# Small transfers of two mixers moved from a shared pair of DMA queues to GpSimd's alone, with their consumers one step later

## The chip, the cores and the metric

The kernel runs on one core of a Trainium2 chip. The metric is the time of one execution on the device in microseconds, the median of several runs. A profile of one execution goes with it: the instructions of every engine with their times, the DMA transfers, and what each engine waited for.

## The reference

The program computes two layers of a decoder trunk for one sequence of 256 tokens of width 2048, in float32. Cut to what matters here:

```python
def reference(x, ...):
    for l in range(DEPTH):                       # DEPTH = 2
        h = rms_norm(x, mix_norm[l])
        h = mixer_ab(h, ...) if l % 2 == 0 else mixer_c(h, ...)
        x = x + h
        h = rms_norm(x, ffn_norm[l])
        x = x + conv_ffn(h, ffn_w_up[l], ffn_conv_w[l], ffn_conv_b[l], ffn_w_down[l])
    return x

def mixer_ab(h, w_in, ...):                      # gMLP heads and HGRN2 heads side by side
    u, v, q, f, i, g = jnp.split(h @ w_in, cuts, axis=-1)
    ...
    return jnp.concatenate([y_a, y_b], axis=-1) @ w_out

def mixer_c(h, w_in, ...):                       # attention with forgetting, 16 heads
    q, k, v, g, f = jnp.split(h @ w_in, ..., axis=-1)
    ...
    return o @ w_out

def conv_ffn(h, w_up, conv_w, conv_b, w_down):
    z = h @ w_up
    z = sum(conv_w[j] * zp[:, j:j + seq] for j in range(CONV_WIDTH)) + conv_b
    a, b = jnp.split(z, 2, axis=-1)
    return (jax.nn.silu(a) * b) @ w_down
```

Nearly all the arithmetic is in the projections `h @ w`. The weights, over 400 MB, are read once.

## The kernel before, in words

**Weights.** Every projection streams its weights in blocks of 512 KB. `weights` (calls `three`, a DMA on SP's queue at L181, and `halves`) brings a block into `w`. ScalarE then writes its rounded half `wh` (L175), VectorE the rest `wl` (L176). The matmuls use both halves of weights and of activations, three products in place of one, which keeps float32's accuracy. Four buffers of `w` and three each of `wh` and `wl` turn over (two more of each in the feed-forward parts), so SP's queue and the two engines work a few blocks ahead of TensorE.

**Steps.** `project_four` (L311 to L313) and `project_tok` (L292 to L294) take two of 16 slices of the model's width for each weight block: 12 matmuls, one *step*. At each step they call `tick`, which moves every running generator one `yield` on. All other work is written as generators: they wait a number of steps with bare `yield`s and then record their instructions. `LAG = 6` is the usual number of steps between a block's transfers and its first reader. `depth` limits how many generators run at once; the others wait in `queue`. The recorded program goes through a scheduler, which sets each engine's order within the dependencies and the extra ones that `held` and `tied` add ("not before this weight split", "not before this matmul").

**Turned blocks.** `project_four` gives tokens on the partitions and features along the row; what follows needs the reverse. `blocks` (L324) transposes 32 x 32 squares with two instructions of VectorE into `tmp`, and `moves` (L331) puts the squares into their places with 16 DMAs of 32 KB within SBUF, from `tmp` to the block's destination. `transposed` does both. The 16 DMAs alternate between SP's queue, where the weights also are, and GpSimd's. A queue issues in order, so a transfer that waits for `tmp` holds up what stands behind it.

**Who uses them.** In `mixer_ab`: `gates` (two blocks `turn`, from the projection f, for the hgrn heads), `gated` (two blocks written into `o`), `spatial` (two blocks `turn`, from the projection u), and `add_four` (four blocks `dst`, the rows of the output projection, added to `xT`). In `mixer_c`: queries and keys of four groups (eight blocks `turn`, read by `attend` at L949), `gate` (four), and `add_four` again (four). In `ffn` every block `zt` goes the same way. Between gates and output, `hgrn` (one generator for each of eight heads) keeps ScalarE and VectorE busy with short instructions while TensorE streams the projections q and i.

**Also on GpSimd's queue**: the copies `ar` (L283, reversed activations for the projection i), and in `mixer_c` the store `cd` (L928) and four loads `cb` (L934), which spread the sums of the forget gates over the partitions; `attend` reads `cb` at L958 and L960.

**Feeding the next part.** `add_four`'s generator adds the turned row to `xT` and calls `nxt.feed`, which makes the activations of the next norm. The last row (`q == 3`) waits two steps less than the others, as the feed-forward part needs it soon. In the rows 1 and 2 of `mixer_ab` (`halves == 2`) the second half of the 16 transfers is issued one step after the first.

Of the kernel before, what the change touches and what calls it, by code (L numbers as in the profile page):

```python
# [25 lines left out]
LAG = 6  # L26
# [27 lines left out]
def tile_trunk(ctx: ExitStack, tc: tile.TileContext, x, pp_d, cst_d, mlev_d, msk_d,  # L54
               w_v, w_f, w_g, w_i, w_q, w_u, w_abo, w_cf, w_cqkv, w_cg, w_co, w_up, w_dn, spw_d, spb_d, out):
    nc = tc.nc
# [259 lines left out]

    def transposed(src, tmp, dst, queues=(nc.sync, nc.gpsimd)):

        blocks(src, tmp)
        moves(tmp, dst, queues)  # L320
# [5 lines left out]

    def moves(tmp, dst, queues=(nc.sync, nc.gpsimd), rows=range(4)):
        n = 2 * BLK
        for a in rows:
            for b in range(4):  # L330
                queues[(a + b) % len(queues)].dma_start(dst[BLK * b:BLK * (b + 1), :, a * n:(a + 1) * n],  # L331
                                  tmp[BLK * a:BLK * (a + 1), b * 4 * n:(b + 1) * 4 * n]
                                  .rearrange("p (m r) -> p m r", m=4))
# [125 lines left out]

    def add_four(q, ps, z, tmp, dst, nxt, halves=1):  # L460
        for T in range(2):
            SC.activation(z[:, T], ps[T], AF.Copy)
        blocks(lambda T: z[:, T], tmp)
        moves(tmp, dst, rows=range(4 // halves))

        def rest():
            if halves == 2:
                yield
                moves(tmp, dst, rows=range(2, 4))
            for _ in range(LAG - 2 * (q == 3)):  # L470
                yield
            for i in range(4):
                m = 4 * q + i
                held(V.tensor_tensor(xT[m], xT[m], dst[:, i], ALU.add), "wl")
                nxt.feed(m)
                if q < 3 or i % 2:
                    yield
            if q == 3:
                for _ in range(WAIT):
                    yield  # L480
                yield from nxt.finish_tok()

        queue.append(rest())


    def mixer_ab(norm):
# [106 lines left out]
        ps = bank()  # L593
# [29 lines left out]
        def gates(j, z):  # L623

            for _ in range(LAG):
                yield
# [15 lines left out]
        for j in range(2):  # L642
# [4 lines left out]
            t = hp.tile([P, 1024], F32, tag="o", name=nm("turn"), bufs=2)  # L647
            transposed(lambda T: z[:, T * 512:(T + 1) * 512], tmp, t.rearrange("p (m t) -> p m t", m=4))
            queue.append(gates(j, t))
# [118 lines left out]
        def gated(j):  # L768
# [15 lines left out]
            for _ in range(2 * (j == 0)):  # L784
                yield
            moves(tmp, t.rearrange("p (m t) -> p m t", m=4))
            for _ in range(LAG - 1):
                yield
# [22 lines left out]
        def spatial(j, z):  # L811
            for _ in range(LAG):
                yield
# [9 lines left out]
        for j in range(2):  # L823
# [4 lines left out]
            t = hp.tile([P, 1024], F32, tag="tok", name=nm("turn"), bufs=2)  # L828
            transposed(lambda T: z[:, T * 512:(T + 1) * 512], tmp, t.rearrange("p (m t) -> p m t", m=4))
            depth[0] = 4  # L830
# [14 lines left out]
        for q in range(4):  # L845
# [12 lines left out]
            if q == 0:  # L858
                depth[0] = 2
            add_four(q, ps, z, tmp, dst, nxt, 2 if q in (1, 2) else 1)  # L860
        es.close()
# [4 lines left out]
    def mixer_c(norm):  # L866
# [127 lines left out]
        def flat(t):  # L994
            return t.rearrange("p t c -> p (t c)")

        def heads(t):
            return flat(t).rearrange("p (m t) -> p m t", m=4)

        for g in range(CH // 4):  # L1000
            qkv = []
            ss = hp.tile([P, 2, 2, LANE // 4], F32, tag="ss", name=nm("ss"), bufs=2)[..., 0:4]
            for j in range(3):
# [12 lines left out]
                if j < 2:  # L1016
# [5 lines left out]
                    t = piece("turn", 4)  # L1022
                    transposed(lambda T: z[:, T], flat(piece("tmp", 2)), heads(t))
                    z = heads(t)
# [8 lines left out]
        def gate(q, z):  # L1033
# [7 lines left out]
            for _ in range(2 * (q < 2)):  # L1041
                yield
            moves(tmp, heads(t))
            for _ in range(LAG - 2 * (q == 3)):
                yield
# [24 lines left out]
    def ffn(l, norm, last):  # L1070
# [69 lines left out]
        def add_y(q, finish):  # L1140
            tmp, zt = room()
            near = last and q == 2
            transposed(lambda T: y[:, T, q * 512:(q + 1) * 512], tmp, zt,
                       (nc.sync, nc.gpsimd, SC) if near else (nc.sync, nc.gpsimd))

# [155 lines left out]
```

## Time and profile before

| | us |
|---|---|
| median of 3 runs | 2288.69 |
| lowest and highest | 2287.63, 2288.85 |
| span of the profiled execution, first to last instruction | 2287.3 |
| TensorE (PE) busy | 2280.8 |
| weight loads into TensorE (PEld) | 1893.5 |
| VectorE (DVE) busy | 1559.8 |
| ScalarE (ACT) busy | 1309.6 |
| GpSimd (POOL) busy | 361.2 |

The profile gives a span but no time of its own for the whole execution; the difference between the median and the span is 1.4 us. "PE pm L311" is a matmul of TensorE at line 311 that writes the tile `pm`. SP is the engine whose queue issues most of the DMAs; "SPq" and "POOLq" are the sequencers of SP and GpSimd. In the timeline each row has the start in us from the span's start, the duration, and in brackets the idle time of the engine before it with what ended it. In the view of waits the numbers are the total, the count and the longest.

### The profile page before, as it was taken

The page shows a single profiled execution, that of the slowest core. Times are in us where ns is not written, and L with a number is a line of the kernel's source. Part 1 is how long each engine was busy: PE and PEld are TensorE (multiplying, and loading weights), DVE is VectorE, ACT ScalarE, POOL GpSimd, SP SyncE. Part 2 cuts the span into 40 slices and gives each one's busy share as a digit, 9 for nine tenths or more (in the row PEclk, how much of TensorE's full clock was granted, in tenths as well). Part 3 has the DMA queues.
Part 4 walks back from the last instruction along what each step waited for, and adds up shares of the span by engine and source line. Part 5 has one row for each costly group of instructions (what it writes and reads, how often), then busy time and mean ns, then how long its engine had stood idle before and what let it go on. Part 6 is the DMA issues. An engine that isn't in the chain of part 4 may idle for free.

```text
span 2287.3 us, 32261 instructions
## 1 busy us (share of the span) xinstructions
PE 2280.8 (100%) x10832; PEld 1893.5 (83%) x10832; DVE 1559.8 (68%) x2309; ACT 1309.6 (57%) x1980; POOL 361.2 (16%) x662
## 2 busy tenths in 40 slices
PE   9999999999999999999999999999999999999999
PEld 8888888888888888888888888888888888888887
DVE  7788767777467656766875675767776476657766
ACT  7677756666456445654565555655665465456642
POOL 0121221212012002111111111211211012012102
PEclk9999999999999999999999999999999999999999
DMA  8655767778667667776666655777777677667765
GB/s 288 195 169 160 215 199 235 238 216 234 193 208 221 206 201 213 220 213 186 213 227 203 194 177 181 220 224 242 225 217 218 195 216 210 209 205 216 223 204 174
DMA packets 489415, 480.45 MB, mean 210 GB/s; under 512 B 114112, under 2 KB 457168, under 8 KB 489120
## 3 DMA queue, kind: packets, MB, share of 16 engines
q1 hardware_dynamic: 467040, 453.54, 64.2%
q0 software_dynamic: 20480, 22.50, 4.3%
q10 hardware_dynamic: 1728, 2.35, 0.3%
q8 instruction: 85, 1.39, 0.3%
q14 instruction: 82, 0.67, 0.1%
HBM read 435.24 MB, written 2.11 MB: 191 GB/s over the span
## 4 chain that ended last, share of the span: by engine, by line
PE 97%; DVE 2%; ACT 1%; issue 0%; SPq 0%; DMA 0%; DVEq 0%; ACTq 0%
PE pm L311 26%; PE pm L312 26%; PE pm L313 26%; PE pm L292 4%; PE pm L294 4%; PE pm L293 4%; PE pm L193 1%; PE pm L266 1%; PE pm L217 1%; DVE wl L176 0%; PE pm L269 0%; ACT wh L175 0%; DVE kq L701 0%; PE px L955 0%; SPq L331 0%
## 5 line engine op out<-in xcount | busy, mean ns | idle before, releaser
L176 DVE TENSOR_TENSOR wl<-w,wh 128x1024 fp32r<-128x1024 f32 (+1 forms) x820 | 996.9, 1219 | 637.0 <-ACT wh L175 629.3
L175 ACT ACTIVATE wh<-w 128x1024 fp32r<-128x1024 f32 (+1 forms) x820 | 862.5, 1054 | 786.0 <-PE pm L313 552.3
L311 PE MATMUL pm<-wh,a 128*128 128x512 f32 x1728 | 674.4, 390 | 0.0
L312 PE MATMUL pm<-wl,a 128*128 128x512 f32 x1728 | 672.5, 389 | 0.0
L313 PE MATMUL pm<-wh,a 128*128 128x512 f32 x1728 | 672.5, 389 | 0.0
L331 POOL DMA_DIRECT2D zt<-tmp x413 | 223.5, 549 | 1201.6 <-DVE tmp L324 1089.8
L313 PEld LDWEIGHTS pm<-wh,a 128*128 128x128 f32 x1728 | 324.4, 188 | 67.4
L312 PEld LDWEIGHTS pm<-wl,a 128*128 128x128 f32 x1728 | 324.4, 188 | 67.3 <-DVE wl L176 0.5
L311 PEld LDWEIGHTS pm<-wh,a 128*128 128x128 f32 x1728 | 324.4, 188 | 67.1
L311 PE MATMUL pm<-wh,hid 128*128 128x512 f32 x688 | 267.6, 389 | 0.0
L312 PE MATMUL pm<-wl,hid 128*128 128x512 f32 x688 | 267.6, 389 | 0.0
L313 PE MATMUL pm<-wh,hid 128*128 128x512 f32 x688 | 267.6, 389 | 0.0
L331 POOL DMA_DIRECT2D turn<-tmp x160 | 86.7, 550 | 504.5 <-DVE tmp L324 256.7
L292 PE MATMUL pm<-wh,a 128*128 128x512 f32 x416 | 165.2, 397 | 0.0
L294 PE MATMUL pm<-wh,a 128*128 128x512 f32 x416 | 162.1, 390 | 0.0
L293 PE MATMUL pm<-wl,a 128*128 128x512 f32 x416 | 162.0, 389 | 0.0
L311 PEld LDWEIGHTS pm<-wh,hid 128*128 128x128 f32 x688 | 129.2, 188 | 26.9
L313 PEld LDWEIGHTS pm<-wh,hid 128*128 128x128 f32 x688 | 129.2, 188 | 26.8
L312 PEld LDWEIGHTS pm<-wl,hid 128*128 128x128 f32 x688 | 129.2, 188 | 26.7
L1105 ACT ACTIVATE conv<-zt,pp 128x256 f32<-128x256 f32 x176 | 95.9, 589 | 26.1 <-DMA zt<-tmp 22.2
L324 DVE STREAM_TRANSPOSE tmp<-z 128x512 f32<-128x512 f32 x120 | 83.4, 704 | 18.9 <-ACT z L1091 18.4
L294 PEld LDWEIGHTS pm<-wh,a 128*128 128x128 f32 x416 | 78.1, 188 | 16.6
(244 smaller groups left out, 2075.6 us busy)
## 6 DMA issues: line engine op xcount, KB each, us to landing
w<-in_w_up SPq DMA_DIRECT2D x352, 512.0 KB, 4.4
w<-in_w_dn SPq DMA_DIRECT2D x176, 512.0 KB, 4.5
w<-in_w_cqkv SPq DMA_DIRECT2D x96, 512.0 KB, 4.3
w<-in_w_abo SPq DMA_DIRECT2D x32, 512.0 KB, 4.6
w<-in_w_cg SPq DMA_DIRECT2D x32, 512.0 KB, 4.3
w<-in_w_co SPq DMA_DIRECT2D x32, 512.0 KB, 4.3
zt<-tmp SPq DMA_DIRECT2D x414, 32.0 KB, 2.7
zt<-tmp POOLq DMA_DIRECT2D x413, 32.0 KB, 2.5
```

What stands on the lines that cost most here:

```text
L175: r = deep["wh"] = SC.activation(wh, w, AF.Copy)
L176: deep["wl"] = V.tensor_tensor(wl, w, wh.bitcast(F32), ALU.subtract)
L193: PE.matmul(ps[g][T], a[:, o + T * P:o + (T + 1) * P], t[:, i * 512:(i + 1) * 512], start=k + i + j == 0, stop=k + i == KT - 1 and j == 2)
L292: PE.matmul(ps[T], ah, h, start=k + i == 0, stop=False)
L293: PE.matmul(ps[T], ah, l, start=False, stop=False)
L294: deep["last"] = PE.matmul(ps[T], al, h, start=False, stop=k + i == KT - 1)
L311: PE.matmul(ps[T], ah, h, start=not begun and k + i == ks[0], stop=False)
L312: PE.matmul(ps[T], ah, l, start=False, stop=False)
L313: deep["mm"] = deep["last"] = PE.matmul(ps[T], al, h, start=False, stop=not more and k + i == ks[-1] + 1)
L324: V.transpose(tmp.rearrange("p (b m i t) -> p b m i t", b=4, m=4, t=2)[:, :, :, :, T], src(T).rearrange("p (m b j) -> p b m j", m=4, b=4))
L331: queues[(a + b) % len(queues)].dma_start(dst[BLK * b:BLK * (b + 1), :, a * n:(a + 1) * n], tmp[BLK * a:BLK * (a + 1), b * 4 * n:(b + 1) * ...
L1105: held(SC.activation(c, z, AF.Identity, bias=pp[:, cb:cb + 1], scale=w(2)))
```

## The change

A name `ONE` stands for GpSimd's queue alone and `TWO` for the pair. In both mixers every turned block uses `ONE`, except the last row of each output projection and the last `gate` block (`q == 3`), which keep `TWO`. The feed-forward blocks keep `TWO`, too. `moves` loses its argument `rows`, and `add_four` its `halves`: all 16 transfers are issued together. The first reader of `gates`, `gated`, `spatial`, `gate` and `add_four` waits one step more; for `q == 3` the number stays what it was (6 - 2 = 4, now 6 + 1 - 3 = 4). The readers of queries and keys have no such count and are not changed.

```diff
-    def transposed(src, tmp, dst, queues=(nc.sync, nc.gpsimd)):
+    ONE, TWO = (nc.gpsimd,), (nc.sync, nc.gpsimd)
+
+    def transposed(src, tmp, dst, queues=TWO):
...
-    def moves(tmp, dst, queues=(nc.sync, nc.gpsimd), rows=range(4)):
+    def moves(tmp, dst, queues=TWO):
         n = 2 * BLK
-        for a in rows:
+        for a in range(4):
...
-    def add_four(q, ps, z, tmp, dst, nxt, halves=1):
+    def add_four(q, ps, z, tmp, dst, nxt):
...
-        moves(tmp, dst, rows=range(4 // halves))
+        moves(tmp, dst, ONE if q < 3 else TWO)
 
         def rest():
-            if halves == 2:
-                yield
-                moves(tmp, dst, rows=range(2, 4))
-            for _ in range(LAG - 2 * (q == 3)):
+            for _ in range(LAG + 1 - 3 * (q == 3)):
                 yield
...
         def gates(j, z):
-            for _ in range(LAG):
+            for _ in range(LAG + 1):
                 yield
...
-            transposed(lambda T: z[:, T * 512:(T + 1) * 512], tmp, t.rearrange("p (m t) -> p m t", m=4))
+            transposed(lambda T: z[:, T * 512:(T + 1) * 512], tmp, t.rearrange("p (m t) -> p m t", m=4), ONE)
             queue.append(gates(j, t))
...
-            moves(tmp, t.rearrange("p (m t) -> p m t", m=4))
-            for _ in range(LAG - 1):
+            moves(tmp, t.rearrange("p (m t) -> p m t", m=4), ONE)
+            for _ in range(LAG):
                 yield
...
         def spatial(j, z):
-            for _ in range(LAG):
+            for _ in range(LAG + 1):
                 yield
...
-            transposed(lambda T: z[:, T * 512:(T + 1) * 512], tmp, t.rearrange("p (m t) -> p m t", m=4))
+            transposed(lambda T: z[:, T * 512:(T + 1) * 512], tmp, t.rearrange("p (m t) -> p m t", m=4), ONE)
             depth[0] = 4
             queue.append(spatial(j, t))
...
-            add_four(q, ps, z, tmp, dst, nxt, 2 if q in (1, 2) else 1)
+            add_four(q, ps, z, tmp, dst, nxt)
...
-                    transposed(lambda T: z[:, T], flat(piece("tmp", 2)), heads(t))
+                    transposed(lambda T: z[:, T], flat(piece("tmp", 2)), heads(t), ONE)
                     z = heads(t)
...
-            moves(tmp, heads(t))
-            for _ in range(LAG - 2 * (q == 3)):
+            moves(tmp, heads(t), ONE if q < 3 else TWO)
+            for _ in range(LAG + 1 - 3 * (q == 3)):
                 yield
```

More of the change, by code (lines that the diff above doesn't have):

```diff
@@ L1143, in add_y @@
             transposed(lambda T: y[:, T, q * 512:(q + 1) * 512], tmp, zt,
-                       (nc.sync, nc.gpsimd, SC) if near else (nc.sync, nc.gpsimd))
+                       TWO + (SC,) if near else TWO)
             def rest():
```

## The prediction

> **What bounds the kernel now.** I read the page first: the shares of part 1, the granted clock and the chain that ended last.
>
> ```profile
> span 2287.3 us, 32261 instructions
> PE 2280.8 (100%) x10832; PEld 1893.5 (83%) x10832; DVE 1559.8 (68%) x2309; ACT 1309.6 (57%) x1980; POOL 361.2 (16%) x662
> PEclk9999999999999999999999999999999999999999
> PE 97%; DVE 2%; ACT 1%; issue 0%; SPq 0%; DMA 0%; DVEq 0%; ACTq 0%
> L175 ACT ACTIVATE wh<-w 128x1024 fp32r<-128x1024 f32 (+1 forms) x820 | 862.5, 1054 | 786.0 <-PE pm L313 552.3
> ```
>
> TensorE is busy all the time at full clock, and 97% of the chain is matmuls. The 820 weight blocks give a mean step of 2287.3/820 = 2.8 us. ScalarE's copy of a weight block (1.05 us) mostly waits for TensorE to give a buffer back, so weights run ahead of their use. A kernel in this state can gain only the time in which TensorE stands still, so the second view is who TensorE waited for:
>
> ```profile
> PE px L681 <- ACT o L753: 1.1, 1, 1.1
> PE warm L144 <- DVE ones L84: 1.1, 1, 1.1
> PE pm L312 <- DVE wl L176: 0.6, 1, 0.6
> ```
>
> Those are all the waits that the view finds: 2.8 us in the whole span, one of them the start. The changed program gives TensorE the same instructions in the same order, so no matmul is added or removed. The time can differ only by waits like these, taken away or new.
>
> Third, the chain in order of time around the wait for `wl`, the only one that a moved transfer stands behind:
>
> ```profile
> 336.50 0.72 DVE tmp L324
> ...
> 337.24 0.60 SPq L331
> ...
> 338.54 1.95 SPq L331
> ...
> 343.12 0.60 SPq L331
> ...
> 343.81 4.01 DMA w<-in_w_abo
> ...
> 347.91 1.07 ACT wh L175
> ...
> 349.00 1.24 DVE wl L176
> ...
> 350.28 0.50 PE pm L312
> ```
>
> This is the end of the second row of the first output projection. SP's queue holds the eight transfers until `tmp` is written (337.22), issues them until 343.72, and only then fetches weights. They land 4 us later, pass ScalarE and VectorE, and TensorE has run dry.
>
> **The change, part by part.** One block of 16 transfers, as it is now, with the weight pipeline beside it (the timeline at the first row of the same projection):
>
> ```profile
> 325.49 1.05 ACT L175 ACTIVATE wh<-w 128x1024 fp32r<-128x1024 f32 x1
> ...
> 326.36 5.12 SPq L331 DMA_DIRECT2D dst<-tmp  x8
> ...
> 326.57 1.23 DVE L176 TENSOR_TENSOR wl<-w,wh 128x1024 fp32r<-128x1024 f32 x1 [0.23 <-ACT wh L175]
> 326.63 4.33 POOL L331 DMA_DIRECT2D dst<-tmp  x8 [27.95 <-DVE tmp L324]
> ...
> 330.23 0.39 PE L311 MATMUL pm<-wh,ya 128*128 128x512 f32 x1
> ```
> ```profile
> DMA to landing us min/median/max: 1.8/2.2/4.2
> ```
>
> The last row is the view of the tile `dst`. *Off SP:* 23 blocks lose 8 issues each there (18 of `turn`, 2 of `o`, 3 of `dst`), 184 x 5.12/8 = 118 us of SP's time. SP is not what ends last except in the pocket above, so only that counts: the 0.6 us wait, and the 0.1 us by which the matmul behind it is longer (0.50 against 0.39). I take -0.7. If SP is late there for another reason the gain is 0; it can't be more, as the wait is no longer.
>
> *Onto GpSimd:* an issue there takes 4.33/8 = 0.54 us, so 16 take 8.7 us. The last landing is at first issue + 15 x 0.54 + 2.2 = +10.3 us: 336.9 for the block above, where SP's last now lands at 326.36 + 7/8 x 5.12 + 2.2 = 333.0. That is 3.9 us later, against one step (2.8 us) that the consumers are given. Each block thus loses about 1.1 us of margin. Who is queued behind: on GpSimd the next blocks, which come 11 us or more apart, and the four `cb` loads (below); the `ar` copies keep their place between blocks that don't touch. On ScalarE and VectorE the split of the next weights stands behind a consumer that waits. In the changed program's order the consumers with a step more stand mostly one or two weight blocks further back, so they need not wait. If one does, the reserve pays: in the rows above `wl` ends at 327.80 for a matmul at 330.23, a reserve of 2.4 us against 1.1. I take 0.
>
> *The hgrn stage*, where ScalarE and VectorE have most to do besides weights, and where the gates of heads 4 to 7 move into the work of the first heads:
>
> ```profile
> 99.39 5.92 SPq L331 DMA_DIRECT2D turn<-tmp  x8
> 99.65 4.33 POOL L331 DMA_DIRECT2D turn<-tmp  x8 [20.93 <-DVE tmp L324]
> 107.18 0.54 ACT L98 ACTIVATE lf<-turn 128x128 f32<-128x128 f32 x2
> ...
> 112.79 1.04 ACT L175 ACTIVATE wh<-w 128x1024 fp32r<-128x1024 f32 x1
> ```
> ```profile
> 108.28 0.35 DVE L637 TENSOR_SCALAR kq<-kq,gm 128x256 f32<-128x256 f32 x1
> ...
> 117.42 1.22 DVE L176 TENSOR_TENSOR wl<-w,wh 128x1024 fp32r<-128x1024 f32 x1
> ...
> 124.28 1.43 DVE L176 TENSOR_TENSOR wl<-w,wh 128x1024 fp32r<-128x1024 f32 x1
> ```
> ```profile
> 121.02 0.50 PE L292 MATMUL pm<-wh,a 128*128 128x512 f32 x1
> ...
> 126.63 0.39 PE L292 MATMUL pm<-wh,a 128*128 128x512 f32 x1
> ```
>
> The block lands at 99.65 + 10.3 = 110.0; its first reader now stands behind the weight copy that starts at 112.79, so nothing waits for it. What moves is work: 16 sigmoids on ScalarE (16 x 0.27 = 4.3 us, from the pair in 0.54) and 4 x 0.35 = 1.4 us on VectorE, some two steps later. Lower end 0, upper end all of it on the path, 5.7 us. The `wl` of 117.42 ends 2.4 us before its matmul (121.02), more than VectorE's 1.4; the one of 124.28 only 0.9 us before 126.63, but by then the gates are past. I take 0, being nearer to the first row. The 1.1 us wait of L681 for `o` L753, further on, is between two heads and no transfer is in it: I leave it, with -1.1 as its lower end and the same again as its upper.
>
> *The first heads of attention.* All 16 `turn` issues now precede the loads of `cb`:
>
> ```profile
> 1152.15 4.33 POOL L331 DMA_DIRECT2D turn<-tmp  x8 [6.65 <-DVE f L920]
> 1156.47 0.51 POOL L928 DMA_DIRECT2D cd<-fc  x1
> 1158.44 2.18 POOL L934 DMA_DIRECT2D cb<-cd  x4 [1.46 <-DMA cd<-fc]
> ```
> ```profile
> DMA to landing us min/median/max: 9.1/11.1/14.1
> ```
> ```profile
> 1170.89 0.35 DVE L958 SCALAR_TENSOR_TENSOR sc<-px,ct,cb 128x128 f32<-128x128 f32 x1 [0.63 <-PE px L955]
> ```
> ```profile
> 1175.72 0.50 ACT L98 ACTIVATE sc<-sc,mxs 128x256 f32<-128x256 f32 x1
> ```
> ```profile
> 1177.00 0.66 PE px L977 x6
> ```
>
> Eight more issues put `cb` at 1158.44 + 4.3 = 1162.7 and its landing (9.1 at the least, view of the tile) at 1171.8, so the reader of 1170.89 waits 0.9 us. The exponential ends at 1176.2, 0.8 us before TensorE's transposes: some 0.1 to 0.2 us get through. With the median landing of 11.1 it would be 2.1 us more. I take +0.3, between 0 and 2.2.
>
> *No cost:* the keys' turned blocks of later groups land 4 us later too, but their heads start after a whole projection of values (8 steps, 22 us). The last row of each mixer keeps both queues and its four steps. `add_four`'s middle rows send all 16 at once instead of in two halves a step apart; their readers had that step already.
>
> [...] Beside the issues on GpSimd at 326.63 VectorE runs `wl` at 326.57, and eight take 4.33 us, as at 99.65. One block shows a pause:
>
> ```profile
> 1275.48 0.55 POOL L331 DMA_DIRECT2D turn<-tmp  x1 [44.96 <-ACT wh L175]
> 1278.56 3.78 POOL L331 DMA_DIRECT2D turn<-tmp  x7 [2.52 <-issue]
> ```
>
> [...]
>
> **The sum.** 2287.3 - 0.7 + 0 + 0.3 = 2286.9 us of span. The median of the three runs is 2288.69, 1.4 us above the profiled span, so 2288.3 us. That is a gain of 0.02%. 0.2% (4.6 us) is about what a measurement of this kernel can tell from no change.
>
> **The rivals.** *First, every wait goes*, L681's too, because ScalarE and VectorE are shuffled around it and `cb` is in time: 2288.3 - 1.1 - 0.3 = 2286.9. For it: the order on both engines differs throughout the hgrn stage. Against it: nothing in the edit is aimed at that wait. *Second, SP is no better off*: weights at 343.81 are late for want of a buffer and not of the queue; then -0.7 is lost, 2289.0. Against it: the chain goes through SP's eight issues without a break.
>
> *Third, slower: the hgrn stage.* The moved 5.7 us of gate work meets a reserve that is already spent (0.9 us at 126.63) and passes through: 2288.3 + 5.7 = 2294.0. It decides once TensorE loses more than 5.0 us there (4.6 beyond the median of before, and the 0.4 of the forecast's gain), that is when nearly nine tenths of the work finds no idle time on its engine. Against it: ScalarE is at 57%, and two steps later is where weights have 2.4 us.
>
> *Fourth, GpSimd's issues falter.* If the pause of 2.5 us comes in many blocks, the last landing is at +12.8 us and a reader waits up to 2.5 us for it. Where the reserve is 2.4 us almost nothing of that gets through. Where it is 0.9, 1.6 us does; two blocks in the hgrn stage and one at the heads, 3 x 1.6 = 4.8, make 2293.1. [...]
>
> **How the numbers follow.** The forecast and its near neighbours (2287.5 to 2289.5) get 0.65, the first rival 0.12, the second 0.06, the third 0.09, the fourth 0.08. The predicted time is 2288.3. Downwards the first rival, with 0.7 us for the runs' own spread, gives 2286.2. Upwards L681's wait doubled (1.1) and `cb` at its median landing (1.9) give 2291.3, and half of the fourth rival's price 2290.7; I close at 2292.0 and leave the third and the worst of the fourth outside. Faster by over 0.2% needs 4.6 us where only 2.8 us of waits exist: 0.02. Slower by over 0.2% is the third rival and a little of the fourth: 0.10. Within: 0.88.
>
> **What would show it.** Right: TensorE's waits hold no `wl` near 350 us; SP issues no small transfers in the mixers but the last rows'; GpSimd shows groups of 16 in about 8.7 us. A wait of some 1 us of VectorE's L958 line (its number moves) for `cb` would confirm the attention term. Wrong: new TensorE waits between 110 and 240 us (third rival), or groups of 16 that take over 11 us (fourth). The prediction fails if TensorE waits at a place where I counted on ScalarE's or VectorE's reserve.

## The result, and the profile after

The changed kernel takes 2291.77 us (median of 19 runs, 2290.84 to 2293.10); the kernel before took 2287.66 us beside it (19 runs, 2286.77 to 2289.09). The ratio is 1.0018, with a 95% interval of 1.0012 to 1.0023: slower by 4.1 us. The forecast was 2288.3 us and a gain of 0.4 us. The profiled execution took 2293.1 us with a span of 2291.3 us, 4.0 us more than the profiled span of before, so the two traces show the whole loss.

The page of the changed kernel, its shares, its granted clock, and the group of GpSimd's small transfers (count | busy us, mean ns | idle before them and who ended it):

```profile
span 2291.3 us, 32057 instructions
PE 2282.2 (100%) x10832; PEld 1893.9 (83%) x10832; DVE 1558.3 (68%) x2309; ACT 1310.0 (57%) x1980; POOL 459.0 (20%) x846
PEclk9999999999999999999999999999999999999999
L333 POOL DMA_DIRECT2D turn<-tmp x304 | 164.9, 550 | 432.1 <-DVE tmp L326 176.7 <-ACT wh L175 90.1 <-issue 47.2
```

TensorE has the same 10832 matmuls, in the same order, and still does nothing but them. GpSimd issues 184 transfers more (846 instructions against 662), at the 0.55 us that one took before. What TensorE waited for:

```profile
PE px L680 <- ACT o L752: 1.6, 2, 1.3
PE pm L312 <- DVE wl L176: 1.6, 2, 0.9
PE warm L144 <- DVE ones L84: 1.1, 1, 1.1
PE px L976 <- ACT sc L98: 0.9, 3, 0.6
```

5.2 us instead of 2.8. The view does not say where. Since the order of the matmuls is the same in the kernels of the table below (nine of 10832 differ in `queue_only`), the start of each matmul can be subtracted from the start of the same one before. That gives the places, and the table under the experiments: -0.9 us near 349 us, as forecast; +1.2 near 1011 us, in the feed-forward part, which the change does not touch; +1.8 at the first heads (1168 to 1184 us); +1.5 at the end of the third gate block of the second mixer (1475 to 1486 us).

These are the places in the timeline of the changed kernel (start, duration, engine, line; in brackets the idle time before and what ended it; rows of GpSimd, ScalarE and VectorE):

```profile
991.28 2.71 POOL L333 DMA_DIRECT2D zt<-tmp  x5 [17.43 <-DVE tmp L326]
996.22 1.63 POOL L333 DMA_DIRECT2D zt<-tmp  x3 [2.23 <-issue]
...
1002.85 1.10 ACT L1104 ACTIVATE conv<-zt,pp 128x256 f32<-128x256 f32 x2 [4.08 <-DMA zt<-tmp]
...
1161.21 2.32 POOL L333 DMA_DIRECT2D turn<-tmp  x4 [1.35 <-DMA turn<-tmp]
1164.24 0.51 POOL L927 DMA_DIRECT2D cd<-fc  x1 [0.72 <-DMA turn<-tmp]
1168.58 2.18 POOL L933 DMA_DIRECT2D cb<-cd  x4 [3.83 <-DMA cd<-fc]
...
1175.67 0.35 DVE L957 SCALAR_TENSOR_TENSOR sc<-px,ct,cb 128x128 f32<-128x128 f32 x1 [2.51 <-DMA cb<-cd]
...
1441.80 5.41 POOL L333 DMA_DIRECT2D turn<-tmp  x10 [11.01 <-ACT yc L378]
1447.83 1.63 POOL L333 DMA_DIRECT2D turn<-tmp  x3 [0.61 <-DMA turn<-tmp]
1450.04 1.63 POOL L333 DMA_DIRECT2D turn<-tmp  x3 [0.58 <-DMA turn<-tmp]
...
1464.27 6.55 POOL L333 DMA_DIRECT2D turn<-tmp  x12 [12.60 <-ACT yc L378]
1471.70 0.55 POOL L333 DMA_DIRECT2D turn<-tmp  x1 [0.88 <-DMA turn<-tmp]
1474.75 1.63 POOL L333 DMA_DIRECT2D turn<-tmp  x3 [2.50 <-issue]
...
1480.10 1.21 ACT L378 ACTIVATE yc<-turn 128x256 fp32r<-128x256 f32 x2 [1.66 <-DMA turn<-tmp]
```

Two things are to be seen. First, an ordinary block of 16 (1441.80) doesn't go out in 8.7 us: after ten issues GpSimd waits for a transfer of its own to land, then again, and has issued the last at 1451.67. The compiled program makes it wait: in the trace GpSimd's transfers carry eight semaphores in turn, and none is issued before the one eight places ahead of it has landed. By the landing events of all 23 blocks of 16, the last transfer lands 12.0 to 16.2 us after the first issue, 13.65 us in the middle; the forecast had 10.3.

Second, two of the blocks shown hold a pause of 2.2 to 2.5 us that ends with "issue", that is, with nothing that the profile shows: at 994 us and at 1472 us. Behind the first, ScalarE's convolution waits for `zt`; behind the second, its `yc` for `turn`; and behind both stands the copy of the next weights. At 994 us the delay is longer than the pause of 2.23 us: the three transfers behind it go out when SP is back at the weights, take 3.0 to 5.0 us each, and the block's last landing is 11.3 us after its first issue; in the kernel before it is 6.5 us (991.60 to 998.08). Such pauses stood in the trace of before, too. These are two of its five:

```profile
491.34 0.55 POOL L331 DMA_DIRECT2D zt<-tmp  x1 [17.43 <-DVE tmp L324]
494.39 3.80 POOL L331 DMA_DIRECT2D zt<-tmp  x7 [2.51 <-issue]
...
904.77 1.63 POOL L331 DMA_DIRECT2D zt<-tmp  x3 [17.43 <-DVE tmp L324]
908.77 2.71 POOL L331 DMA_DIRECT2D zt<-tmp  x5 [2.37 <-issue]
```

Counting GpSimd's transfers from the start of the program, they come after numbers 113, 219, 326, 432 and 538 in the kernel before, and after 113, 219, 325, 432, 538, 644 and 750 in the changed one: every 106 or 107 transfers. The kernel before issues 626 of them and has its five pauses at 492, 906, 1276, 1612 and 2027 us; the changed one issues 810, and the pauses come at 338, 645, 994, 1280, 1472, 1683 and 2115 us (the one at 1683 us lasts 2.09 us, and the view puts it down to a landing).

### The profile page after: what moved, and what is told of

It is laid out like the page before. It is cut to its first block, busy times and chain, and to the rows that moved or that the text cites. A ratio compares the mean times of both kernels' runs of the same rounds, so it can differ in the third digit from the quotient of the medians.

```text
span 2291.3 us, 32057 instructions
## 1 busy us (share of the span) xinstructions
PE 2282.2 (100%) x10832; PEld 1893.9 (83%) x10832; DVE 1558.3 (68%) x2309; ACT 1310.0 (57%) x1980; POOL 459.0 (20%) x846
## 3 DMA queue, kind: packets, MB, share of 16 engines
q10 hardware_dynamic: 1728, 2.35, 0.3%
## 5 line engine op out<-in xcount | busy, mean ns | idle before, releaser
L333 POOL DMA_DIRECT2D turn<-tmp x304 | 164.9, 550 | 432.1 <-DVE tmp L326 176.7
```

## The experiments

The theory after the result: the losses come from the place of the pauses, which is set by the number of transfers on GpSimd ahead of them, and at the first heads from `cb`, which now stands behind 16 slow issues. The rivals: the one step that the readers were given does harm; the new traffic beside the weights, or the slow landing of the blocks, costs by itself; the order of the engines' work does.

In the table, each number is the time that TensorE lost (or, negative, won) in a stretch, in us: the shift of its matmuls' starts against the profiled execution of before. The last column is the median of the runs, less that of the kernel before on the same chip. The places of a row come from one execution. The profiled execution of before spans 2287.3 us, and the spans of before beside the experiments have medians of 2286.2 to 2286.5. So a row need not add up to its last column: each profiled execution stands off its kernel's median, that of before by about 1 us.

| kernel | start to 100 | hgrn, to 320 | near 349 | to 500 | near 1011 | first heads | gates, 1460 to 1505 | output rows, to 1600 | median |
|---|---|---|---|---|---|---|---|---|---|
| the change | -0.1 | +0.4 | -0.9 | +0.1 | +1.2 | +1.8 | +1.5 | 0 | +4.1 |
| step_only | -0.4 | -1.5 | -0.4 | 0 | 0 | 0 | 0 | 0 | -0.9 |
| queue_only | +0.1 | -1.0 | -0.9 | +0.4 | +1.2 | +0.9 | +1.1 | +1.7 | +3.2 |
| ab_only | -0.6 | +0.4 | -0.9 | 0 | +1.6 | 0 | 0 | 0 | +2.2 |
| c_only | -0.2 | 0 | -0.9 | 0 | 0 | +0.6 | 0 | 0 | +2.0 |
| thirteen_more | -0.2 | +0.4 | -0.9 | +0.7 | +0.5 | 0 | +1.4 | 0 | +3.3 |
| keys0_two | -0.4 | +0.4 | -0.9 | 0 | +1.1 | 0 | +4.8 | 0 | +7.0 |
| keys0_21 | +0.7 | +0.4 | -0.9 | +0.5 | +0.3 | 0 | +1.7 | 0 | +3.8 |
| before_72 | +2.3 | +3.8 | -0.4 | 0 | +1.3 | 0 | 0 | 0 | +4.0 |
| more_32 | +0.8 | +0.5 | -0.9 | 0 | 0 | 0 | 0 | 0 | +0.6 |
| keys0_40 | +1.2 | +0.4 | -0.9 | +0.4 | 0 | 0 | +0.1 | 0 | +0.8 |
| rows_ab | +0.1 | 0 | -0.9 | 0 | 0 | +5.0 | 0 | +2.1 | +5.7 |

**The step alone, and the queue alone.** First the readers' extra step with both queues kept:

```
-    ONE, TWO = (nc.gpsimd,), (nc.sync, nc.gpsimd)
+    ONE = TWO = (nc.sync, nc.gpsimd)
```

> The changed kernel with both queues kept for every block; the readers keep their extra step. Theory (late landings on GpSimd cost the time, not the step): SP holds the weights back again while it issues the eight transfers, so a block lands some 6 us after its first issue, no reader waits, and the time is that of the kernel before, 2287.7, within 0.8 us; in the profile the wait at the end of the second output row (0.9 us) is back and the losses near 1011, 1177 and 1486 us are gone. Rival (the step and the new order on ScalarE and VectorE cost it): 1 to 3 us slower than before.

2287.24 us, ratio 0.9997 (0.9988 to 1.0006). Of TensorE's waits only this one and that at the start are in it:

```profile
PE pm L312 <- DVE wl L176: 0.2, 1, 0.2
```

The step does no harm; the wait for `o` in the hgrn stage, which the prediction left alone, is not in this profile, and a third of the one near 349 us remains. Then the queue with the old step (the output rows 1 and 2 of the first mixer are then read a step earlier than before, as their `halves` are gone):

```
-            for _ in range(LAG + 1):
+            for _ in range(LAG):
...
-            for _ in range(LAG + 1 - 3 * (q == 3)):
+            for _ in range(LAG - 2 * (q == 3)):
```

> The changed kernel with GpSimd's queue alone but the readers at their old step. Theory (a block of 16 lands 12 to 16 us after its first issue, because weights now stream beside it): readers meet it a step earlier, so the time is at least that of the changed kernel, 2291.8, up to 2297; blocks of 16 still take 12 to 16 us to land. Rival (the step is the cause): 2287.7.

2291.30 us, ratio 1.0016 (1.0007 to 1.0024), a little under the 2291.8 expected. The whole loss comes with the queue. Without the step there is one loss more, 1.7 us in the output rows of the second mixer, and one less, in the hgrn stage; in the sum its worth is within the intervals. The loss in the output rows has no pause in it:

```profile
1547.35 5.40 POOL L333 DMA_DIRECT2D turn<-tmp  x10 [13.31 <-DVE tmp L326]
...
1556.23 2.17 POOL L333 DMA_DIRECT2D turn<-tmp  x4 [1.13 <-DMA turn<-tmp]
...
1563.38 1.10 DVE L473 TENSOR_TENSOR x<-x,turn 128x256 f32<-128x256 f32 x3 [2.91 <-DMA turn<-tmp]
```

So the slow landing of a block can cost by itself, where its reader does not have the extra step.

**One mixer at a time.** `ab_only` keeps the change in the first mixer, `c_only` in the second; of each, one of the edits (in `c_only` the output rows of the first mixer are on both queues again, but without `halves`: their 16 transfers are issued together):

```
-                    transposed(lambda T: z[:, T], flat(piece("tmp", 2)), heads(t), ONE)
+                    transposed(lambda T: z[:, T], flat(piece("tmp", 2)), heads(t), TWO)
```
```
-            transposed(lambda T: z[:, T * 512:(T + 1) * 512], tmp, t.rearrange("p (m t) -> p m t", m=4), ONE)
+            transposed(lambda T: z[:, T * 512:(T + 1) * 512], tmp, t.rearrange("p (m t) -> p m t", m=4), TWO)
```

> The change in the first mixer alone; the second as before. Theory of the count (GpSimd's queue pauses some 2.4 us after every 106th transfer, wherever that falls): the transfers up to the first feed-forward part are those of the changed kernel, so the pause after number 325 falls in the same block near 994 us and costs 1.2 us again: 2287.7 - 0.9 (output row) + 0.4 (hgrn stage) + 1.2 = 2288.4. If the loss near 1011 us was chance: 2287.2.

> The change in the second mixer alone; the first as before. The first heads wait for the loads that stand behind 16 transfers, 1.8 us; the feed-forward part before it has the pauses of the kernel before, which cost nothing. The pause that fell into the third gate block near 1472 us now falls some 30 transfers later or, by count, into the first gate block near 1420. Theory of the count: without a pause the third gate block lands in time and the 1.4 us near 1486 do not appear: 2287.7 + 1.8 - 0.2 = 2289.3. Rival (the late landing alone does it, without the pause): 2290.7.

2290.33 us (1.0010, interval 1.0001 to 1.0019) and 2290.13 us (1.0008, 0.9999 to 1.0017). With the first mixer alone the count of transfers up to 1011 us is that of the change, and so are the pause at 993.39 us and the loss. With the second mixer alone the count is another: no pause at 994 us and no loss there; and the pause of the gates falls into the first gate block (1423.91 us), where it costs nothing, with no loss at 1475 to 1486 us. So both losses go with the pause. Both kernels took longer than expected (2288.4 and 2289.3 us). `c_only` also shows -0.9 us near 349 us although SP issues eight transfers of that block as before; and in `before_72` below, whose mixers are those of before, TensorE waits 0.26 us there instead of 0.62. So that wait differs between executions, and how much of the -0.9 us belongs to the change is not shown. For `ab_only` this would account for most of the difference: without it, 2288.1 + 0.4 + 1.6 = 2290.1 us. In `c_only` the end after the last matmul is 1.3 us longer than before's in this profile; why stays open.

**Moving the pauses.** Transfers that nothing needs, ahead of all else, shift the count. The first try, with 13:

```
+    for i in range(13):
+        nc.gpsimd.dma_start(spare.tile([P, LANE], F32, tag=f"spare{i}", name=f"spare{i}"), ones[:, 0:LANE])
```

> The change, with 13 pointless transfers (128 x 64 values to a scratch in DRAM) added on GpSimd's queue at the very start, where it has nothing to do for 70 us. It leaves out nothing. Theory: GpSimd pauses some 2.4 us after its transfers number 113, 219, 325, 432, 538, 644 and 750, by count alone. With 13 more ahead, number 325 is the last of a block of eight in the feed-forward (near 973 us) and number 538 the last of the second gate block (near 1451 us), so both pauses fall into idle time of GpSimd. The 1.2 us that TensorE loses at 1011 us and the 1.4 us at 1475 to 1486 us are then gone: 2291.5 - 2.6 = 2288.9 us, faster than the change by doing more. The loss at the first heads (1168 to 1184 us) stays. Rival: those two losses come from the traffic of the weights or from the order of work, and the pause only falls beside them: both stay, 2291.5 us.

2291.39 us, ratio 1.0014 (1.0005 to 1.0023): the forecast gain did not come. The rows of GpSimd:

```profile
972.62 4.33 POOL L337 DMA_DIRECT2D zt<-tmp  x8 [20.01 <-issue]
...
1464.57 4.33 POOL L337 DMA_DIRECT2D turn<-tmp  x8 [14.51 <-issue]
```

The pauses came after numbers 325 and 538 again, which are now the last of a block. But the idle time up to the next block does not hide them: that idle time now ends with "issue", and the block begins some 2 us late (1464.57, against 1464.27 in the change, whose matmuls are 1.7 us later by then). The pause is paid at the next issue, whenever that is. So the third gate block was late as before, and lost 1.4 us as before. The block at 972.62 us shows it most plainly, with 20.01 us of idle time where the block before it (948.28 us) has 17.43; near 1011 us 0.5 us of the loss remained.

Then the keys of the first heads on both queues again, and the same with 21 transfers ahead:

```
-                    transposed(lambda T: z[:, T], flat(piece("tmp", 2)), heads(t), ONE)
+                    transposed(lambda T: z[:, T], flat(piece("tmp", 2)), heads(t),
+                               TWO if g == 0 and j == 1 else ONE)
```

> The change, but the turned keys of the first group of heads go over both queues again, eight on each. Theory: the cb loads are then issued near 1158 to 1160 us instead of 1168.6, and TensorE's loss at 1168 to 1184 us (1.8 us in the change's profile) is gone. GpSimd has issued eight transfers less by the gates, so its pause number 538 moves from the third gate block to number 546 of the old count, in the middle of the fourth block (near 1490 us): the 1.4 us at 1475 to 1486 us go, and up to 2.4 us may come near 1495 to 1500 us. The 1.2 us at 1011 us stay. Between 2288.3 (nothing new) and 2290.7. Rival: the heads lose through ScalarE's and VectorE's new order, not through cb; then the loss stays there, 2290 to 2291.5.

> Both at once: the first group's turned keys on both queues, and 21 pointless transfers at the start. The pauses then fall behind number 304 of the old count (between two blocks of the feed-forward) and behind number 525 (between the second and the third gate block). If the three losses named are all that the change costs, each by its own cause, this version loses none of them: 2291.5 - 1.2 - 1.4 - 1.0 to 1.8 = 2287.1 to 2287.9 us, the time of the kernel before or a little under it. If it stays at 2289 us or more, a cause is missing from the account.

2295.09 us (1.0033, 1.0021 to 1.0045) and 2291.84 us (1.0016, 1.0007 to 1.0025). In both the loss at the first heads is gone, as expected: the four `cb` loads are issued from 1159.06 and 1159.67 us on instead of 1168.58. (These two runs alone don't decide it, as `thirteen_more`, with the keys as in the change, lost nothing there either; the starts of the reader, in the part on the prediction, do.) `keys0_21` put the pause at the start of the third gate block once more, by the same wrong assumption as with 13, and lost 1.7 us there. `keys0_two` has the pause in the fourth gate block, and there it cost 4.8 us, twice its length. The timeline of that kernel, GpSimd, ScalarE and TensorE, and below it the same stretch by windows (us, busy time and instructions of each engine, granted clock, DMA share, GB/s):

```profile
1483.90 2.71 POOL L333 DMA_DIRECT2D turn<-tmp  x5 [12.49 <-ACT wh L175]
1488.83 1.63 POOL L333 DMA_DIRECT2D turn<-tmp  x3 [2.23 <-issue]
...
1493.64 0.39 PE L313 MATMUL pm<-wh,yc 128*128 128x512 f32 x1
1496.76 0.50 PE L311 MATMUL pm<-wh,yc 128*128 128x512 f32 x1 [2.73 <-ACT yc L378]
...
1499.22 0.63 PE L312 MATMUL pm<-wl,yc 128*128 128x512 f32 x1
```
```profile
1485.00:1493.00 8.00, 8.00 (x37) 6.62 (x36) 3.66 (x4) 2.12 (x2) 3.23 (x6) 1.00 0.70 198
1493.00:1497.00 4.00, 1.27 (x6) 0.77 (x5) 0.26 (x1) 0.94 (x2) 0.00 (x0) 1.00 1.04 315
1497.00:1501.50 4.50, 4.50 (x13) 3.33 (x13) 4.20 (x6) 3.27 (x5) 0.00 (x0) 0.62 0.01 2
```

The three late transfers went out at 1488.83 us together with the weights, for which SP was free again by then (315 GB/s in the stretch behind), and the last landed at 1495.76 us, 5.8 us after its issue. TensorE waited 2.73 us for the `yc` made of it. And then, over 4.5 us, its granted clock was 0.62, and a matmul took 0.63 us instead of 0.39: that is most of the other 2 us. A mean of 0.62 over 4.5 us is half the clock for 4.5 x (1 - 0.62) / 0.5 = 3.4 us, an estimated cost of 1.7 us; from 1497.98 to 1501.35 us eight matmuls start 0.38 to 0.43 us apart instead of 0.23, 1.6 us more in all. From 1501.50 to 1506.00 us the granted clock is 1.00 again. Here a wait of 2.73 us stood ahead of the halved clock, in `before_72` and `rows_ab` below shorter ones.

**The pause in the kernel before.** If the place of the pause decides, the kernel before must lose at 1011 us too, once 72 transfers stand ahead of it; nothing else is changed:

```
+    for i in range(72):
+        nc.gpsimd.dma_start(spare.tile([P, LANE], F32, tag=f"spare{i}", name=f"spare{i}"), ones[:, 0:LANE])
```

> The kernel before, not changed at all but for 72 pointless transfers (128 x 64 values to a scratch in DRAM) on GpSimd's queue at the start. Theory: the pause comes by the count of GpSimd's transfers and is paid at the next issue. In the kernel before, number 219 falls at 906.4 us and costs nothing; with 72 more ahead, number 325 falls in the block of eight at 991 to 996 us, where the changed kernel had it. TensorE should lose some 0.5 to 1.2 us near 1011 us in this kernel too, although its mixers are untouched: 2288.1 + 0.5 to 1.2 = 2288.6 to 2289.3 us. Another pause falls in the first gate block (near 1418 us), where one cost nothing with the change in the second mixer alone. Rival: the loss at 1011 us belongs to the change (its order of work, or its traffic); then nothing is lost there, 2288.1 us.

2292.43 us (1.0017, 1.0007 to 1.0026). GpSimd and ScalarE near 1011 us (the times are 6 us later than in the change, since this run lost more before):

```profile
997.53 2.71 POOL L335 DMA_DIRECT2D zt<-tmp  x5 [17.43 <-DVE tmp L328]
1002.47 1.63 POOL L335 DMA_DIRECT2D zt<-tmp  x3 [2.23 <-issue]
...
1009.25 1.10 ACT L1109 ACTIVATE conv<-zt,pp 128x256 f32<-128x256 f32 x2 [4.22 <-DMA zt<-tmp]
```

The same pause after the fifth transfer, the same wait of the convolution, and the same loss, 1.3 us, in a kernel whose mixers are untouched. The rest of its time was not expected: 2.3 us at the start, where the 72 transfers are, and 3.8 us behind the second `turn` block of `spatial` (first issue at 296.65 us), into which another pause fell. TensorE waited 0.86 and 0.76 us there, and then had half its clock for 3.4 us (windows as above):

```profile
313.90:317.30 3.40, 3.40 (x10) 2.64 (x9) 3.10 (x6) 3.24 (x5) 0.00 (x0) 0.50 0.79 232
```

The profiled execution is the slowest of its eleven (2296.07 us against the median of 2292.43), and only it and one other list a mean clock below 1.000; so the part that half the clock cost, 1.7 us, is not in the median.

**The change with harmless pauses.** 32 transfers ahead put them into a feed-forward block at 905 us, as in the kernel before, and into the first gate block, as in `c_only`; the edit is that of 13, with 32.

> The change, with 32 pointless transfers at the start (13 were too few: they put two pauses behind the last transfer of a block, and the pause was paid by the first of the next). Theory: the pauses then fall behind numbers 293 (the block at 904 us, where the kernel before has one for nothing), 400 (keys) and 506 (the first gate block, harmless with the change in the second mixer alone), so that the losses at 1011 us (1.2) and at 1475 to 1486 us (1.4) are gone: 2291.5 - 2.6 = 2288.9 us. The heads may lose 0 to 1.8 us of it as before. Rival: the third gate block costs 1.3 us through its landing time of 14 us without any pause; then the loss stays, 2290.2 us.

2288.98 us, ratio 1.0003 (0.9995 to 1.0012): with 32 pointless transfers more, the change stands 0.6 us above the kernel before instead of 4.1. TensorE's waits, without that of the start:

```profile
PE px L684 <- ACT o L756: 1.6, 2, 1.3
...
PE pm L217 <- ACT wh L175: 0.2, 1, 0.2
```

No loss at 1011 us, at the heads or at the gates is left, and no `wl` wait. The blocks of 16 still land as late as in the change (12.0 to 15.7 us after their first issue): with the extra step that costs nothing here. The pause at the second `turn` block of `spatial`, which cost `before_72` 3.8 us, is in this kernel too, after the block's first transfer as there (295.72 us), and costs nothing; here the whole block is on GpSimd's queue, and its reader has a step more. TensorE's last matmul starts 0.2 us later than in the profile of before; 0.8 us are lost at the start, where the 32 transfers are.

Both remedies together, the keys of the first heads on both queues and 40 transfers ahead, which puts the pauses behind the same transfers after the heads:

> The change with the first group's turned keys on both queues and 40 pointless transfers at the start, so that the pauses fall behind the same transfers as with 32 and no change of the keys (285 in the feed-forward, 400 in the keys, 506 in the first gate block). Theory: all three losses are gone, as 2291.5 - 1.2 - 1.4 - 1.0 to 1.8 = 2287.1 to 2287.9 us, and 2293.2 us of the version with 21 transfers less show what the place of a pause is worth. If it stays at 2289 us or more, a cause is missing from the account.

2289.16 us (1.0004, 0.9995 to 1.0013). The three losses are gone. It stays above 2289 all the same; the profile shows 1.2 us at the start, more than with 32, which I had not counted and which would account for it. `keys0_two`, the same change of the keys without transfers ahead, stands 7.0 us above before, this one 0.8. (The 2293.2 us that the expectation names is the span of the profile of `keys0_two`; the version with 21 transfers, `keys0_21`, took 2291.84 us.)

**Only the first mixer's output rows.** The part for which a gain was forecast, rows 0 to 2 with their 24 transfers and nothing else; `add_four` gets the queues and the step as arguments:

```
-            add_four(q, ps, z, tmp, dst, nxt)
+            add_four(q, ps, z, tmp, dst, nxt, ONE, LAG + 1)
...
-            transposed(lambda T: z[:, T * 512:(T + 1) * 512], tmp, t.rearrange("p (m t) -> p m t", m=4), ONE)
+            transposed(lambda T: z[:, T * 512:(T + 1) * 512], tmp, t.rearrange("p (m t) -> p m t", m=4), TWO)
```

> One part alone: only the first mixer's output rows 0 to 2 go to GpSimd with their readers a step later (24 transfers moved), all else as before. It should show the gain forecast for the change, the 0.6 to 0.9 us at 349 us, by itself, and move the pauses by 24: number 219 to a block at 839 us, number 325 to one near 949 us. By the theory nothing else is lost unless a pause of 2.4 us meets a thin reserve: 2287.2 to 2288.1 us. Rival: blocks of 16 with a landing time of 12 to 15 us cost by themselves here, where two follow each other directly; then 2288.5 us or more with a wait between 326 and 400 us.

2294.09 us (1.0028, 1.0018 to 1.0037), slower than the whole change. The -0.9 us near 349 us are there, as in `c_only`, and blocks of 16 that follow each other cost nothing between 326 and 400 us. But 24 transfers more put pause 325 here:

```profile
1151.36 2.71 POOL L333 DMA_DIRECT2D turn<-tmp  x5 [6.65 <-DVE f L919]
1156.30 1.63 POOL L333 DMA_DIRECT2D turn<-tmp  x3 [2.23 <-issue]
1157.92 0.51 POOL L927 DMA_DIRECT2D cd<-fc  x1
1164.19 2.18 POOL L933 DMA_DIRECT2D cb<-cd  x4 [5.76 <-DMA cd<-fc]
```

These are the keys of the first heads, in code that is as before, and TensorE loses 5.0 us at them. Not through `cb`: ScalarE waits for the late block, and the copy of the next weights behind it. TensorE waits 2.09 and 0.77 us for the weights, and then again has half its clock (0.52 in this stretch):

```profile
1165.80 0.49 PE L292 MATMUL pm<-wh,a 128*128 128x512 f32 x1 [2.09 <-ACT wh L175]
1167.06 0.50 PE L293 MATMUL pm<-wl,a 128*128 128x512 f32 x1 [0.77 <-DVE wl L176]
```
```profile
1167.70:1171.20 3.50, 3.50 (x10) 2.71 (x9) 2.36 (x2) 1.87 (x3) 0.00 (x0) 0.52 1.02 369
```

Number 432 falls into the third output row of the second mixer (1550.58 us) and costs 2.1.

**Why a block takes 14 us to land.** All 16 on SP's queue instead of GpSimd's; this holds the weights back while they are issued. Its times are so far from the others that it is left out of the table:

```
-    ONE, TWO = (nc.gpsimd,), (nc.sync, nc.gpsimd)
+    ONE, TWO = (nc.sync,), (nc.sync, nc.gpsimd)
```

> The change with all 16 transfers of a block on SP's queue instead of GpSimd's, readers one step later as in the change. Theory: a block on GpSimd takes 12 to 16 us to land because the weights, which SP no longer holds back, stream beside it at 175 to 230 GB/s. Here SP issues no weights during its 16 issues (16 x 0.64 = 10.2 us), so transfers land in 2 to 4 us each and the block in 15 x 0.64 + 2.2 = some 12 us; but the weights come 10 us late, and TensorE runs dry in many of the 23 blocks: over 2297 us. Rival: a train of 16 on one queue is slow by itself, whatever flows beside it; then latencies climb to 5 to 7 us here too and the block takes 14 us or more.

2388.05 us, ratio 1.0435 (1.0421 to 1.0450). From issue to landing, by the view of the tile `turn`: before, after the change, and here:

```profile
DMA to landing us min/median/max: 1.7/2.0/6.3
```
```profile
DMA to landing us min/median/max: 1.8/4.3/6.9
```
```profile
DMA to landing us min/median/max: 1.8/1.9/7.2
```

And the DMA traffic while a block of 16 is under way (last two numbers: share and GB/s), in the changed kernel and here:

```profile
1441.80:1455.50 13.70, 13.70 (x62) 11.35 (x61) 8.23 (x9) 6.43 (x7) 8.67 (x16) 1.00 0.83 242
```
```profile
343.00:354.60 11.60, 11.60 (x53) 9.61 (x52) 6.26 (x7) 4.61 (x6) 0.00 (x0) 1.00 0.33 83
```

With the weights held back (83 GB/s), a train of 16 on one queue lands in 11.5 to 13.2 us (22 of 23 blocks), nearly all of it issue time, at a median of 1.9 us each. With the weights beside it (242 GB/s) the median is 4.3 us. So here the landing is slow with the traffic, not because the 16 are on one queue. The two runs differ in the issuing engine as well, but each queue shows both speeds. The 23rd block of this run (1186.75 us) has the loads of `cb` beside its last seven transfers (280 GB/s from 1192.00 to 1202.60 us), and these take 4.6 to 7.2 us on SP's queue. In the kernel before, the pause at 1276 us sends the last three of a block's eight on GpSimd out after SP's eight, beside the weights (248 GB/s from 1278.50 to 1288.00 us): they take 4.3 to 6.3 us, the five before them 1.8 to 2.5. In the kernel before SP was itself busy with small transfers during a block (eight in 5.12 us at 326.36 us) and issued no weights: the change took the protection away with the load. The price of holding the weights back altogether is 100 us.

## Why the prediction was wrong, point by point

*What bounds the kernel* was right: TensorE, same matmuls, full clock, and only waits could move the time.

*The pocket on SP, -0.7*: the wait is gone as forecast, -0.9 us in the profile. But it is gone in `c_only` too, where SP still issues eight of that block's transfers, and smaller in `before_72`; so the median of before held only part of it, and a gain from the change is not shown.

*One block of 16, last landing at first issue + 15 x 0.54 + 2.2 = +10.3 us*: wrong in both terms. The 2.2 us were the median landing of `dst` in the kernel before, with SP's own issues in place of weights (90 GB/s from 337.50 to 343.70 us); beside the weights it is 4.3 in the median and up to 6.9, and GpSimd waits in each block for its own transfers to land, so that the issues take 9 to 12 us and not 8.7. Measured, 12.0 to 16.2. Yet the cost taken for it, 0, holds for nearly all blocks: `more_32` has these slow blocks and none of the losses. It is the extra step that covers them: `queue_only`, without it, loses 1.7 us at a slow block that has no pause.

*The hgrn stage, 0 (0 to 5.7)*: +0.4, in the wait for `o` (1.6 us for two instead of 1.1 for one). The third rival did not come.

*The first heads, +0.3 (0 to 2.2)*: the mechanism was right, the size was too small by 1.5 us, though inside its bounds; +1.8 in this profile. `cb` was issued at 1168.58 and not at 1162.7, since the issues ahead of it were slow. The reserve was larger than the 0.7 us that I read: over five kernels (`more_32`, `thirteen_more`, `c_only`, `queue_only` and the change), with TensorE's shift taken off, the first `cb` reader starting at 1172.85, 1173.27, 1173.82, 1174.11 and 1175.06 us goes with a loss of 0, 0.02, 0.59, 0.89 and 1.83 us, so that it is late from 1173.24 on, 2.35 us behind its time before (1170.89). The change stands at that edge: the same code lost nothing in `thirteen_more` and `more_32`.

*The pause* is the step that failed. The sum put it at nothing ("I take 0" for the blocks on GpSimd) without a reason other than that one block alone showed it. I quoted that one, at 1276 us, and gave the fourth rival 0.08 with the condition that it comes "in many blocks". It does not: it comes seven times, by the count of GpSimd's transfers. The trace of before held five of them, 106 or 107 transfers apart, and listing GpSimd's rows that end with "issue" would have shown the count. The change adds 184 transfers, so all the pauses fall elsewhere and there are seven, two of them into blocks with thin reserve: 1.2 + 1.5 us, one in code that is not edited. The prediction looked for costs only where instructions were moved. VectorE's work beside the issues is not seen to stretch them: an issue takes 0.55 us in both kernels and none more than 0.67, with VectorE busy for 68% of the span; and the pauses follow the count.

In sum, I forecast the change 0.4 us below the kernel before; with the pauses in harmless places it stood 0.6 above, within the interval of no change and with 0.8 us at the start for the transfers that moved them. The other 3.5 us are the places of two pauses, and the heads, which stand at an edge. The measured 2291.8 us lies inside the range of 2286.2 to 2292.0, but that is partly luck: its upper end was made of a doubled wait at L681 and a late `cb`, or of half the fourth rival's price for pauses in the hgrn stage and at the heads. The first two came to some 2 us above the forecast; the 2.7 us of the two pauses stand at places that the range did not consider.

What stays open: what GpSimd does in the pause (no row shows it); and the 1.3 us at the end of `c_only`.

## What to carry to other kernels

Before transfers are moved onto a queue, list that engine's own idle times in the trace that no instruction explains, count what lies between them, and work out where they fall after the change: everything behind the first moved transfer shifts, also in code that isn't edited. Here the issue slots that small transfers took from the weight queue also kept the weights off the DMA engines while they landed (90 GB/s from 337.50 to 343.70 us in the kernel before, 234 from 337.80 to 352.80 us in the changed one); with the slots gone the median landing went from 2.0 to 4.3 us. And compare a change of this size with a version that only shifts the pauses, or an effect of place is taken for one of the change. And waits of TensorE of 1.6 to 2.9 us in all cost an estimated 1.7 us more than their length in three of these profiles, as 3.4 us at half the clock followed them.

## What the runs showed of the hardware that I had not expected

GpSimd paused for 2.1 to 2.5 us after every 106th or 107th transfer that it issued, the first time after number 113: five times in the kernel before, seven times in the changed one. Where the same count puts them, `thirteen_more` (331.33 us), `before_72` (299.70 and 1002.47 us), `rows_ab` (1156.30 and 1552.97 us), `more_32` (1427.70 us) and `keys0_two` (1488.83 us) show pauses of 2.2 to 2.5 us. The 13 to 72 pointless transfers count like the others, but they too are of 32 KB in 128 pieces of 256 bytes, as are all but five of the program's own on this queue: whether the count goes by transfers, pieces or bytes is not shown. The pause was paid at the next issue and not hidden in idle time: 20.01 us of idle time where the block before has 17.43 (`thirteen_more`, 972.62 us), and idle times that end with "issue" in `thirteen_more` (14.51 us, to 1464.57 us) and `keys0_21` (14.49 us, to 1464.73 us).

Transfers of 32 KB within SBUF took 1.9 us in the median on SP's queue in `sync_only` (83 GB/s of traffic in all while a block was under way). On GpSimd's queue in the changed kernel the median was 4.3 us (242 GB/s), and three beside 248 GB/s in the kernel before took 4.3 to 6.3 us; seven on SP's queue beside 280 GB/s in `sync_only` took 4.6 to 7.2 us.

Half the clock for 3.4 us followed waits of TensorE of 2.73 us (`keys0_two`), of 2.09 and 0.77 us one behind the other (`rows_ab`), and of only 0.86 and 0.76 us (`before_72`); each time by the granted clock an estimated 1.7 us more, half of 3.4. It did not follow a single wait of 1.38 us (`queue_only`, 1567.89 us), nor 0.73 and 0.77 us (`rows_ab`, 1564 us), nor 2.27 and 0.53 us (`sync_only`, 117.52 us; the granted clock stayed at 1.00). So in these traces the length alone does not decide; what does is not shown.
